# State space input of a three-branch trunk: projected channel-major and re-laid through DRAM in place of token-major with every eighth token stationary

## The chip, the cores and the metric

One core of a Trainium2 chip runs the whole kernel in one launch. The metric is the device time of one execution in microseconds (us). A core has five instruction queues: TensorE (PE, matrix products; its weight loads are a row of their own, PEld), VectorE (DVE), ScalarE (ACT), GpSimd (POOL) and SyncE (SP, which here only issues DMA transfers). Each engine works through its own instructions in the order of the program and waits on semaphores for the others.

## The reference

Two layers over 1024 tokens of 1024 channels. Each normalises its input, projects it with one matrix `w_in`, splits the columns among three mixers, gates each mixer's output, and adds the product with `w_out` to the residual. A is sparse attention with a top-256 selection of keys, B a state space layer on 256 of the columns (u), C latent attention. The change concerns u:

```python
proj = h @ w_in[l]
(qa, ka, va, iq, ik, iw, ga, u, gb, cq, ckv, kpe, gc) = jnp.split(proj, points, axis=-1)
ya = dsa_branch(qa, ka, va, iq, ik, iw, ...)
yb = s5_branch(u, ssm_a_re[l], ssm_a_im[l], ssm_b_re[l], ...)   # x_t = a x_(t-1) + B u_t; y = Re(C x) + D u
mixed = concat([ya * silu(ga), yb * silu(gb), yc * silu(gc)], axis=-1)
x = x + mixed @ w_out[l]
```

The 256 columns of u are 16 groups of 16 channels; each group drives a complex state of 64.

## The kernel before, in words

A layer starts by transposing the normalised input h into channel-major tiles, one for each block k of 128 input channels, split into two parts `hh` and `hl` (`h_hi[k]`, `h_lo[k]`, 128 channels x 1024 tokens). Weights arrive as `raw` by SP and are split by POOL into `whi` and `wlo`. Every product is the sum of three matmuls (hi x hi, lo x hi, hi x lo).

The projections run as a list of steps, `STEPS = "L5C6Q7U01234"` (line 52): L, C, Q and U are projections of 256 columns, the digits are gates of 128 columns. Two forms exist.

- Token-major, `proj` and `proj_step` (lines 723 to 754; matmuls on lines 730, 732, 733): a block of 128 tokens of h is the stationary operand, 256 columns of the weight move, and the result `pj` has tokens on the partitions. It takes 8 blocks of tokens x 8 blocks of channels x 3 = 192 matmuls of 256 columns. For step U the stationary block is not 128 neighbouring tokens but every eighth one, `slice(7 - e, 1024, 8)`, so that `pj` has chunk j of 8 tokens on the partitions. `ev_u` (line 763, ACT) copies it to two tiles `us[c]` with the chunk j on the partitions and (group, e, channel) along the row.
- Channel-major, `gates` (line 1122; matmuls of `mm3` on lines 167 to 169): the weight columns are stationary, 512 tokens move, and the result `gt` has channels on the partitions. It takes 2 halves x 8 x 3 = 48 matmuls of 512 columns for 128 columns of weight. A gate then goes by tanh (ACT, line 1132) and a product (DVE, line 1133) to the tile `gate`, is stored to the DRAM scratch `gate_d` (SP, line 1134), and comes back much later as `gin` (line 1238).

Beside this main stream run generators ("sides"). Every step of the main stream calls `tick` with an estimate of its time; a side whose next step is due then writes its instructions at that point of the program. So the order on each engine is set when the program is written, by these estimates. Three sides matter here.

- The selection of A's keys, `topk` (DVE mainly). Near its end a reduction gives `bad` (line 987), one matmul sums it over the partitions into `pb` (line 989), and DVE casts that to `badi` (line 991).
- The state space branch: `s5_tables`, then `s5` (line 356). `static(gh)` makes the tables of one half of the groups: `s5o` and `s5t` (DVE and POOL), small matmuls `tr<-zp,s5bd` and `tr<-s5o,s5bd` (line 397), the kernel `s5k` (line 405, DVE), eight SP transfers `s5m<-s5k` (line 409), and transposes of `s5t` (line 414). Then `chunks(gh)` (line 434) needs u as `U`, partitions (e, channel), rows (group, chunk): eight PE transposes of `us[gh]` (line 441) and two ACT copies (line 442) make it, and 16 small matmuls (line 449; the trace shows two records for each) give `vr` and `vi`, which DVE takes up on lines 457 and 458. `outputs(gh)` follows. The order is static(0), chunks(0), outputs(0) mixed with static(1), chunks(1), outputs(1).
- Attention of A: queries `qA` (DVE, line 1356, from PE transposes on line 1352 of `qa`, which SP loads on line 1346), scores (PE, lines 1360 and 1361), a maximum with the mask (DVE, line 1176), exponentials to `P` (ACT, line 1184), transposes of P (PE, line 1204) and the product with va into `acc_o` (line 1197).

Of the kernel before, what the change touches and what calls it, by code (L numbers as in the profile page):

```python
# [9 lines left out]
F32 = mybir.dt.float32  # L10
# [26 lines left out]
LEAD = 2  # L37
# [53 lines left out]
def hybrid_kernel(ctx, tc, A, out, dbg=None, layers=DEPTH):  # L91
# [31 lines left out]
    def scr(shape, dt, name):  # L123
        """scratch of up to 1, 2 or 4 KB a partition"""
        n = int(np.prod(shape[1:])) * (2 if dt == BF16 else 4)
        if n > 2048:
            return page(shape, dt, name)
        tag, bufs = ("k1", K1) if n <= 1024 else ("k2", K2)
        return sm.tile(shape, dt, tag=tag, name=name, bufs=bufs)
# [11 lines left out]
    # ---------------------------------------------------------------- constants  # L141
# [6 lines left out]
    # ---------------------------------------------------------------- helpers  # L148
# [12 lines left out]
    def rsq(o, x, c, m=1.0):  # L161
        """((x + c) * m) ** -0.5"""
# [8 lines left out]
    def rope(eng, o, x, c, s, t1, t2, dup=1):  # L171
        """x: [128, n, 2, h]; c, s: [128, h]; o: [128, n, dup, 2, h] or, without copies, [128, n, 2, h]"""
# [17 lines left out]
    # ---------------------------------------------------------------- state space branch  # L190
    zp = {}

    def tiny(name, n=8, dt=F32):
        """a slice of a page; the same name is the same place within a layer"""
# [8 lines left out]
    def exp_acc(x, name):  # L203
        """e ** x by 2 ** n and a polynomial; zero below the normal range"""
# [17 lines left out]
    def sincos(x, name):  # L222
# [17 lines left out]
        # quadrant  # L240
# [13 lines left out]
        # signs: sin is negative in quadrants 2, 3; cos in 1, 2  # L254
# [27 lines left out]
    def s5_tables(l, Z):  # L282
        """parameters of a layer: powers of abar, input matrices, rotation; as a generator"""
# [38 lines left out]
        # powers abar ** 0..8  # L322
# [17 lines left out]
        # e ** (8 i th), its powers of two, and the modulus of a chunk  # L340
# [15 lines left out]
    def s5(l, Z, us, yb):  # L356
        """groups 0..7, then 8..15; as a generator. The input must have been projected when sync is passed"""
# [6 lines left out]
        def table(eng, gh, name, e0, mr, mi):  # L364
            """[(group of the pair, state), re/im, pair, e, channel]: abar ** (e0 + e) * m"""
# [7 lines left out]
        def static(gh):  # L373
            """what the parameters give: input and output matrices, Toeplitz blocks, rotation"""
# [7 lines left out]
            # K[tau][c, c'] = Re(C abar ** tau B), both groups of a pair by block-diagonal matrices of input,  # L382
            # then the block Toeplitz matrices [(e c), g, (t c')]
# [17 lines left out]
            # D on the diagonal of tau = 0  # L401
# [15 lines left out]
            # rotation, unit modulus: e ** (8 i th j)  # L417
# [15 lines left out]

        def chunks(gh):
            """chunk inputs [(e c), g, j] and what they bring to the states"""
            h = H[gh]
            h["U"] = U = page([128, 8, 128], F32, "s5U")
            for q in range(2):
                p = ps_tr([128, 4, 128])
                for i in range(4):  # L440
                    T.transpose(p[:, i, :], us[gh][:, 4 * q + i].rearrange("p e c -> p (e c)"), ident)
                S.activation(U[:, 4 * q:4 * q + 4, :], p, AF.Copy)
                yield 1.5
# [25 lines left out]
            # states before each chunk  # L469
# [6 lines left out]
        def outputs(gh):  # L476
            """outputs [j, (t, g, c)], gelu (doubled), transposed to channels x tokens"""
# [30 lines left out]
        while len(us) < 3:  # L508
            yield 1.0
        yield from chunks(0)  # L510
# [7 lines left out]
        # g times the sigmoid of its linear layer (four times that)  # L518
# [25 lines left out]
    # work beside the main stream: generators that yield the time, in us, until their next step  # L544
# [3 lines left out]
    def side(gen, delay=0.0, behind=0):  # L548
        """behind: instructions that go first"""
# [19 lines left out]
    # ---------------------------------------------------------------- layers  # L569
    cq_d = dram.tile([2, 2, 128, 1024], F32, name="cq_d")  # L570
    qa_d = dram.tile([1024, 384], F32, name="qa_d")
    gate_d = dram.tile([8, 128, 1024], F32, name="gate_d")

# [1065 lines left out]
```

## Time and profile before

| | us |
|---|---|
| median of 3 runs | 1357.48 (1355.61 to 1359.18) |
| profiled execution, its span | 1357.0 |
| PE busy in it | 1306.3 |
| DVE busy | 919.6 |
| POOL busy | 681.7 |
| ACT busy | 666.5 |

The span is that of one profiled execution. A row of the timeline gives start, duration, engine, line, operation, output<-input; a number in square brackets is the idle time of the engine just before it, and what released it. A letter q behind an engine's name (SPq) marks the issue of a transfer by that engine's queue. Matmuls are pipelined: the duration of one is longer than the distance to the next, so the distance between starts is what one costs. PEclk in a table of stretches is the granted clock of PE as a share of full speed (1.00 is 2.4 GHz, 0.50 is 1.2 GHz).

### The profile page before, as it was taken

The page shows a single profiled execution, that of the slowest core. Times are in us where ns is not written, and L with a number is a line of the kernel's source. Part 1 is how long each engine was busy: PE and PEld are TensorE (multiplying, and loading weights), DVE is VectorE, ACT ScalarE, POOL GpSimd, SP SyncE. Part 2 cuts the span into 40 slices and gives each one's busy share as a digit, 9 for nine tenths or more (in the row PEclk, how much of TensorE's full clock was granted, in tenths as well). Part 3 has the DMA queues.
Part 4 walks back from the last instruction along what each step waited for, and adds up shares of the span by engine and source line. Part 5 has one row for each costly group of instructions (what it writes and reads, how often), then busy time and mean ns, then how long its engine had stood idle before and what let it go on. Part 6 is the DMA issues. An engine that isn't in the chain of part 4 may idle for free. (4 is left out here: it accounts for less than half of the span.)

```text
span 1357.0 us, 26056 instructions
## 1 busy us (share of the span) xinstructions
PE 1306.3 (96%) x9636; PEld 1153.7 (85%) x9636; DVE 919.6 (68%) x2672; ACT 666.5 (49%) x1521; POOL 681.7 (50%) x1109
## 2 busy tenths in 40 slices
PE   6999999999999999999999899999999999999998
PEld 6987899877788787789999789998777878777998
DVE  4478799698677866731253888978986776587211
ACT  5356621115788666751143674101277966668300
POOL 5987278255327743523158944843751476344400
PEclk8999999999999899999999899999999999999999
DMA  7102222112200001421150014222140100015103
GB/s 247 33 5 75 94 86 70 36 64 93 73 16 27 5 23 48 161 94 25 70 165 1 24 56 125 63 63 65 56 133 11 32 11 18 10 48 195 55 1 125
DMA packets 74849, 88.14 MB, mean 65 GB/s; under 512 B 12960, under 2 KB 62240, under 8 KB 74720
## 3 DMA queue, kind: packets, MB, share of 16 engines
q1 hardware_dynamic: 73568, 82.26, 19.1%
q0 software_dynamic: 1152, 4.19, 0.9%
q8 instruction: 76, 1.25, 0.4%
q14 instruction: 53, 0.43, 0.1%
HBM read 61.14 MB, written 24.12 MB: 63 GB/s over the span
## 5 line engine op out<-in xcount | busy, mean ns | idle before, releaser
L730 PE MATMUL pj<-whi,hh 128*128 128x256 f32 (+1 forms) x736 | 224.6, 305 | 0.9 <-POOL whi L150 0.9
L732 PE MATMUL pj<-wlo,hh 128*128 128x256 f32 (+1 forms) x736 | 223.7, 304 | 1.6 <-POOL wlo L151 1.6
L733 PE MATMUL pj<-whi,hl 128*128 128x256 f32 (+1 forms) x736 | 223.6, 305 | 0.0
L155 POOL TENSOR_TENSOR wlo<-raw,whi 128x1024 fp32r<-128x1024 f32 (+1 forms) x40 | 94.6, 2380 | 145.3 <-PE po L1470 65.8
L732 PEld LDWEIGHTS pj<-wlo,hh 128*128 128x128 f32 x736 | 160.6, 218 | 2.5 <-POOL wlo L151 1.8
L730 PEld LDWEIGHTS pj<-whi,hh 128*128 128x128 f32 x736 | 160.5, 218 | 2.2 <-POOL whi L150 1.2
L733 PEld LDWEIGHTS pj<-whi,hl 128*128 128x128 f32 x736 | 160.1, 218 | 0.3
L1469 PE MATMUL po<-whi,mix 128*128 128x256 f32 x512 | 145.2, 284 | 0.3 <-DVE xn L1556 0.3
L1470 PE MATMUL po<-wlo,mix 128*128 128x256 f32 x512 | 144.7, 284 | 0.0
L1471 PE MATMUL po<-whi,mix 128*128 128x256 f32 x512 | 143.9, 283 | 0.0
L1556 DVE TENSOR_TENSOR xn<-xn,po 128x256 f32<-128x256 f32 x64 | 26.4, 420 | 126.2 <-PE po L1471 126.2
L167 PE MATMUL gt<-hh,whi 128*128 128x512 f32 x256 | 103.9, 406 | 0.0
L169 PE MATMUL gt<-hh,wlo 128*128 128x512 f32 x256 | 102.5, 400 | 0.0
L168 PE MATMUL gt<-hl,whi 128*128 128x512 f32 x256 | 102.5, 400 | 0.0
L922 DVE SCALAR_TENSOR_TENSOR acc<-rl,iw,acc 128x384 f32<-128x384 f32 (+5 forms) x84 | 94.0, 1120 | 12.2 <-ACT rl L917 9.3
L1210 ACT ACTIVATE pt<-s 128x512 f32<-128x512 f32 (+1 forms) x154 | 82.6, 559 | 36.3 <-PE s L1204 30.0
L1469 PEld LDWEIGHTS po<-whi,mix 128*128 128x128 f32 x512 | 98.3, 192 | 0.7 <-DVE xn L1556 0.7
L1470 PEld LDWEIGHTS po<-wlo,mix 128*128 128x128 f32 x512 | 98.3, 192 | 0.0
L1471 PEld LDWEIGHTS po<-whi,mix 128*128 128x128 f32 x512 | 97.7, 192 | 0.0
L1204 PE MATMUL s<-ident,P 128*128 128x128 f32 x588 | 96.5, 281 | 0.6 <-ACT P L1184 0.2
L1184 ACT ACTIVATE P<-P,nb,qsc 128x1024 f32<-128x1024 f32 (+7 forms) x96 | 82.3, 865 | 21.8 <-DVE nb L1182 21.8
L1184 ACT ACTIVATE P<-P,nb,asum 128x1024 f32<-128x1024 f32 (+7 forms) x96 | 82.6, 868 | 17.6 <-DVE nb L1182 17.5
(447 smaller groups left out, 3660.8 us busy)
## 6 DMA issues: line engine op xcount, KB each, us to landing
raw<-in_w_in SPq DMA_DIRECT2D x32, 512.0 KB, 4.6
gate_d<-gate SPq DMA_DIRECT2D x16, 512.0 KB, 2.9
gin<-gate_d SPq DMA_DIRECT2D x16, 512.0 KB, 3.4
raw<-in_w_out SPq DMA_DIRECT2D x16, 512.0 KB, 4.6
x<-in_x SPq DMA_DIRECT2D x8, 512.0 KB, 5.4
cq_d<-cqs SPq DMA_DIRECT2D x16, 256.0 KB, 2.1
cqT<-cq_d POOLq DMA_DIRECT2D x8, 512.0 KB, 5.4
xn<-in_x SPq DMA_DIRECT2D x8, 512.0 KB, 9.3
```

The lines of the kernel that those rows point to most:

```text
L155: (eng or G).tensor_tensor(lo, raw, f(hi), op=ALU.subtract)
L167: T.matmul(ps, lh, rh, start=start, stop=False)
L168: T.matmul(ps, lh, rl, start=False, stop=False)
L169: T.matmul(ps, ll, rh, start=False, stop=stop)
L730: T.matmul(o, hk, hi[:, k, 0:n], start=kh == 0 and i == 0 and k == 0, stop=False, skip_group_check=True)
L732: T.matmul(o, hk, lo[:, k, 0:n], start=False, stop=False, skip_group_check=True)
L733: T.matmul(o, lk, hi[:, k, 0:n], start=False, stop=kh == 1 and k == 3, skip_group_check=True)
L1184: S.activation(Ps[j][:, 0:nk], Ps[j][:, 0:nk], AF.Exp, bias=nb[:, j:j + 1], scale=it["scale"][:, j:j + 1], accum_out=sums[:, j:j + 1])
L1204: T.transpose(p[:, i, :], Ps[j][:, 128 * kt:128 * kt + 128], ident)
L1469: T.matmul(o, mh, hi[:, k, :], start=first and i == 0 and k == 0, stop=False, skip_group_check=True)
L1470: T.matmul(o, mh, lo[:, k, :], start=False, stop=False, skip_group_check=True)
L1471: T.matmul(o, ml, hi[:, k, :], start=False, stop=final and k == 3, skip_group_check=True)
```

## The change

Step U now uses the channel-major form. The body of `gates` becomes a generator, `channels()`, used by the gates and by a new `inputs_s5()`: for each half c of the 256 columns, 48 matmuls of 512 columns give u with channels on the partitions; ACT copies each half of the tokens to a tile `uT` so that the eight tokens of a chunk come apart (position s, then chunk j), and SP stores the tile to a new DRAM scratch `u_d[c]`. The weight for step U is loaded as two blocks of 128 columns (`gate_w`) instead of two halves of 512 input channels; the bytes are the same.

In `s5` a new `inputs(gh)` loads `U` from that scratch by eight SP transfers of 64 KB, one for each position e: 16 partitions (channels) x 8 groups x 128 chunks. Both halves are asked for after static(0) and ahead of chunks(0). `chunks` loses its transposes and copies and the two yields of 1.5 between them; the `us` list holds only numbers of halves that are stored. The argument `sl` of `proj` goes. Comments go as well; they are left out here.

```diff
         def chunks(gh):
             h = H[gh]
-            h["U"] = U = page([128, 8, 128], F32, "s5U")
-            for q in range(2):
-                p = ps_tr([128, 4, 128])
-                for i in range(4):
-                    T.transpose(p[:, i, :], us[gh][:, 4 * q + i].rearrange("p e c -> p (e c)"), ident)
-                S.activation(U[:, 4 * q:4 * q + 4, :], p, AF.Copy)
-                yield 1.5
+            U = h["U"]
...
+        def inputs(gh):
+            H[gh]["U"] = U = page([128, 8, 128], F32, "s5U")
+            src = u_d[gh].rearrange("(g c) (s j) -> c g s j", c=16, s=8)
+            for e in range(8):
+                nc.sync.dma_start(U[16 * e:16 * e + 16, :, :], src[:, :, 7 - e, :])
...
         yield from static(0)
-        while len(us) < 3:
+        while len(us) < 2:
             yield 1.0
+        inputs(0)
+        yield 4.0
+        inputs(1)
         yield from chunks(0)
...
+    u_d = dram.tile([2, 128, 1024], F32, name="u_d")
...
+            elif x == "U":
+                reqs.extend(lambda col=col: gate_w(l, col) for col in (1192, 1320))
...
-        def ev_u(tp, ps):
-            if tp == 0:
-                us.extend(page([128, 8, 8, 16], F32, f"u{c}") for c in range(2))
-            for c in range(2):
-                S.activation(us[c].rearrange("p g e c -> p e g c")[:, 2 * tp:2 * tp + 2],
-                             ps[:, :, 128 * c:128 * c + 128].rearrange("p e (g c) -> p e g c", g=8), AF.Copy)
-            if tp == 3:
-                us.append(True)
...
-        def gates(c):
-            hi, lo, _ = ws.get()
-            g = page([128, 1024], F32, f"gate{c}")
-            for hf in range(2):
-                cs = slice(512 * hf, 512 * hf + 512)
-                ps = ps_s([128, 512], "gt")
-                for k in range(8):
-                    mm3(ps, hi[:, k, :], lo[:, k, :], h_hi[k][:, cs], h_lo[k][:, cs], k == 0, k == 7)
-                    tick(0.64)
+        def channels():
+            hi, lo, _ = ws.get()
+            for hf in range(2):
+                cs = slice(512 * hf, 512 * hf + 512)
+                ps = ps_s([128, 512], "gt")
+                for k in range(8):
+                    mm3(ps, hi[:, k, :], lo[:, k, :], h_hi[k][:, cs], h_lo[k][:, cs], k == 0, k == 7)
+                    tick(0.64)
+                yield hf, cs, ps
+        us = []
+        def inputs_s5():
+            for c in range(2):
+                u = page([128, 8, 128], F32, "uT")
+                for hf, _, ps in channels():
+                    S.activation(u[:, :, 64 * hf:64 * hf + 64], ps.rearrange("p (j s) -> p s j", s=8), AF.Copy)
+                nc.sync.dma_start(u_d[c], u.rearrange("p s j -> p (s j)"))
+                us.append(c)
+        def gates(c):
+            g = page([128, 1024], F32, f"gate{c}")
+            for hf, cs, ps in channels():
...
-                proj(ev_u, sl=lambda e: slice(7 - e, 1024, 8), outer=x not in INNER)
+                inputs_s5()
```

Since the estimates of the sides' due times change, so does the order on the engines. PE's instructions fall from 8534 to 8310. In the first layer, pb stood behind 192 matmuls of U and 12 of gate 0, and stands behind 96 of U and 16 of gate 0.

On PE, where vr and vi of the first half are made, the order of before. Names: s are scores, u_2786 the tile us[0], s5w the input matrices, tr a PSUM tile of transposes; line 1360 and 1361 make a pair.

```order
1636 L414 MATMUL tr<-ident,s5t 128x128 x4
1637 L1352 MATMUL tr<-ident,qa 128x128 x3
1638 L1360 MATMUL s<-ka_hi,qA 128x512
1639 L1361 MATMUL s<-ka_lo,qA 128x512
1640 L441 MATMUL tr<-ident,u_2786 128x128 x4
1641 L1360 MATMUL s<-ka_hi,qA 128x512
1642 L1361 MATMUL s<-ka_lo,qA 128x512
1643 L1360 MATMUL s<-ka_hi,qA 128x512
1644 L1361 MATMUL s<-ka_lo,qA 128x512
1645 L441 MATMUL tr<-ident,u_2786 128x128 x4
1646 L449 MATMUL vr<-s5U,s5w 64x128
1647 L449 MATMUL vi<-s5U,s5w 64x128
```

The same place on PE in the changed kernel (line 1372 is 1360 of before, 1373 is 1361, 450 is 449, 1364 is 1352).

```order
1540 L414 MATMUL tr<-ident,s5t 128x128 x4
1541 L1364 MATMUL tr<-ident,qa 128x128 x3
1542 L1372 MATMUL s<-ka_hi,qA 128x512
1543 L1373 MATMUL s<-ka_lo,qA 128x512
1544 L1372 MATMUL s<-ka_hi,qA 128x512
1545 L1373 MATMUL s<-ka_lo,qA 128x512
1546 L1372 MATMUL s<-ka_hi,qA 128x512
1547 L1373 MATMUL s<-ka_lo,qA 128x512
1548 L450 MATMUL vr<-s5U,s5w 64x128
1549 L450 MATMUL vi<-s5U,s5w 64x128
1550 L450 MATMUL vr<-s5U,s5w 64x128
1551 L450 MATMUL vi<-s5U,s5w 64x128
```

The transposes of u are gone. Five pairs of scores stand ahead of the first row in both. Before, ten pairs in all stood ahead of the last seven of the eight pairs of vr and vi, and two pairs behind them; now all eight follow the eighth pair of scores without a break, and four pairs of scores stand behind them. For the second half, vr and vi stand some 65 instructions earlier in the stream than before.

On SP, the queue around the s5m transfers, before:

```order
69 L409 DMA s5m<-s5k 16x8x32
70 L409 DMA s5m<-s5k 16x8x16
71 L1134 DMA gate_d<-gate_4001 128x1024
72 L1238 DMA gin_4141<-gate_d 128x1024
73 L1238 DMA gin_4143<-gate_d 128x1024
74 L1346 DMA qa<-qa_d 128x384 x2
```

And in the changed kernel:

```order
69 L409 DMA s5m<-s5k 16x8x32
70 L409 DMA s5m<-s5k 16x8x16
71 L1146 DMA gate_d<-gate_3904 128x1024
72 L1250 DMA gin_4044<-gate_d 128x1024
73 L1250 DMA gin_4046<-gate_d 128x1024
74 L439 DMA s5U<-u_d 16x8x128 x16
75 L1358 DMA qa<-qa_d 128x384 x2
```

Sixteen loads (eight for each half) have come in between the gin loads and the qa loads, behind all eight s5m transfers.

## Rows read from the trace of the kernel before

**Rows 1.** Page, part 1: engine, busy us (share of span), instructions.

```profile
PE 1306.3 (96%) x9636; PEld 1153.7 (85%) x9636; DVE 919.6 (68%) x2672; ACT 666.5 (49%) x1521; POOL 681.7 (50%) x1109
```

**Rows 2.** Stretches: us, busy (instructions) of PE, PEld, DVE, ACT, POOL; PEclk; DMA; GB/s.

```profile
202.00:248.00 46.00, 46.00 (x193) 45.97 (x191) 37.90 (x100) 5.18 (x10) 29.58 (x32) 1.00 0.17 52
248.00:300.00 52.00, 52.00 (x233) 42.79 (x233) 46.06 (x188) 8.66 (x14) 21.83 (x21) 1.00 0.16 53
```

**Rows 3.** Timeline of PE: first matmul of U, first gate matmul behind it.

```profile
202.25 0.29 PE L730 MATMUL pj<-whi,hh 128*128 128x256 f32 x1
...
248.40 0.40 PE L167 MATMUL gt<-hh,whi 128*128 128x512 f32 x1
```

**Rows 4.** Timeline of PE: two gate matmuls, six apart, in gate 7.

```profile
194.77 0.39 PE L167 MATMUL gt<-hh,whi 128*128 128x512 f32 x1
...
196.13 0.39 PE L167 MATMUL gt<-hh,whi 128*128 128x512 f32 x1
```

**Rows 5.** Timeline of DVE at the end of the selection; the last in layer 1.

```profile
236.53 0.15 DVE L987 TENSOR_REDUCE bad<-tk_ok 128x1 f32<-128x6 f32 x1
...
251.48 0.15 DVE L991 CAST badi<-pb 1x1 int32<-1x1 f32 x1 [10.80 <-PE pb L989]
...
918.15 0.15 DVE L991 CAST badi<-pb 1x1 int32<-1x1 f32 x1 [10.80 <-PE pb L989]
```

**Rows 6.** Timeline of PE from pb to the transposes of P.

```profile
251.26 0.19 PE L989 MATMUL pb<-consts,bad 128*1 128x1 f32 x2
...
304.86 0.63 PE L414 MATMUL tr<-ident,s5t 128*128 128x128 f32 x4 [2.82 <-DVE qA L1356]
...
312.02 0.39 PE L1360 MATMUL s<-ka_hi,qA 128*128 128x512 f32 x1
...
319.26 0.45 PE L449 MATMUL vr<-s5U,s5w 128*64 128x128 f32 x4
319.53 0.40 PE L449 MATMUL vi<-s5U,s5w 128*64 128x128 f32 x4
...
322.20 0.38 PE L1204 MATMUL tr<-ident,P 128*128 128x128 f32 x2
322.93 0.44 PE L1204 MATMUL tr<-ident,P 128*128 128x128 f32 x2 [0.35 <-ACT P L1184]
```

**Rows 7.** Groups of PE by line: busy us, mean ns, idle before.

```profile
L441 PE MATMUL tr<-ident,u 128*128 128x128 f32 x32 | 4.9, 276 | 0.0
```

**Rows 8.** Stretches behind two idle times of PE, columns as in rows 2.

```profile
307.00:308.00 1.00, 1.00 (x9) 1.00 (x8) 0.86 (x7) 0.00 (x0) 0.77 (x5) 0.50 0.07 16
...
446.00:456.00 10.00, 8.83 (x40) 7.83 (x42) 7.51 (x28) 6.62 (x13) 7.33 (x6) 0.50 0.00 0
```

**Rows 9.** Timeline of DVE: the kernel s5k is finished.

```profile
311.37 0.27 DVE L405 TENSOR_TENSOR s5k<-s5k,zp 16x128 f32<-16x128 f32 x1
```

**Rows 10.** Timeline of SP's queue: two zp loads, s5m, and what follows it.

```profile
262.10 0.43 SPq L290 DMA_DIRECT2D zp<-in_ssm_b_re  x1
262.58 0.43 SPq L290 DMA_DIRECT2D zp<-in_ssm_b_im  x1
...
311.70 5.22 SPq L409 DMA_DIRECT2D s5m<-s5k  x8
...
318.96 0.91 SPq L1346 DMA_DIRECT2D qa<-qa_d  x2
```

**Rows 11.** DMA issues: count, KB each, median us from issue to landing.

```profile
cqT<-cq_d POOLq DMA_DIRECT2D x8, 512.0 KB, 5.4
...
s5m<-s5k SPq DMA_DIRECT2D x4, 64.0 KB, 2.3
...
zp<-in_ssm_b_re SPq DMA_DIRECT2D x2, 64.0 KB, 1.9
```

**Rows 12.** Timeline of PE: the wait ahead of the slow stretch.

```profile
446.48 0.48 PE L1197 MATMUL acc_o<-pt,va 128*64 128x128 f32 x2 [1.98 <-DVE gin L1227]
```

More of the change, by code (lines that the diff above doesn't have):

```diff
@@ L613, in gate_w @@
         return raw, 128
-    R_U, R_IQ, R_K = [(1192, 1448)], [(512, 768)], [(384, 512), (768, 808), (2088, 2120)]
+    R_IQ, R_K = [(512, 768)], [(384, 512), (768, 808), (2088, 2120)]
     R_L, R_CQ, R_QA = [(1960, 2088), (0, 128)], [(1704, 1960)], [(128, 384)]
@@ L619, in in_weights @@
     def in_weights(l):
-        cols = dict(K=R_K, I=R_IQ, L=R_L, C=R_CQ, Q=R_QA, U=R_U)
+        cols = dict(K=R_K, I=R_IQ, L=R_L, C=R_CQ, Q=R_QA)
         reqs = []
@@ L721, in proj_halves, with proj_step @@
                             evac(2 * hf + p, pss[p])
-        def proj_step(ps, t0, kh, hi, lo, n, sl=None):
+        def proj_step(ps, t0, kh, hi, lo, n):
             for i in range(2):
                 t = t0 + i
-                cs = slice(128 * t, 128 * t + 128) if sl is None else sl(t)
+                cs = slice(128 * t, 128 * t + 128)
                 for k in range(4):
@@ L734, in proj_step, with proj @@
             tick(n / 100.0)
-        def proj(evac, sl=None, tps=range(4), outer=True):
+        def proj(evac, tps=range(4), outer=True):
             if not outer:
@@ L741, in proj @@
                     for kh in range(2):
-                        proj_step(ps, 2 * tp, kh, *w[kh], sl)
+                        proj_step(ps, 2 * tp, kh, *w[kh])
                     evac(tp, ps)
@@ L751, in proj @@
                     ps = pss[tp]
-                    proj_step(ps, 2 * tp, kh, hi, lo, n, sl)
+                    proj_step(ps, 2 * tp, kh, hi, lo, n)
                     if kh == 1:
                         evac(tp, ps)
-        us = []
-        def ev_u(tp, ps):
-            if tp == 0:
-                us.extend(page([128, 8, 8, 16], F32, f"u{c}") for c in range(2))
-            for c in range(2):
-                S.activation(us[c].rearrange("p g e c -> p e g c")[:, 2 * tp:2 * tp + 2],
-                             ps[:, :, 128 * c:128 * c + 128].rearrange("p e (g c) -> p e g c", g=8), AF.Copy)
-            if tp == 3:
-                us.append(True)
         iraw = {}
@@ L1117, in ev_g5 @@
             qa_out(tp, 2, ps)
-        mixf = {}
-        def gates(c):
+        def channels():
             hi, lo, _ = ws.get()
-            g = page([128, 1024], F32, f"gate{c}")
             for hf in range(2):
@@ L1130, in gates @@
                     tick(0.64)
+                yield hf, cs, ps
[7 more added lines that the diff above has]
+                us.append(c)
+        mixf = {}
+        def gates(c):
+            g = page([128, 1024], F32, f"gate{c}")
+            for hf, cs, ps in channels():
                 th = scr([128, 512], F32, "th")
```

## The prediction

> **What bounds the kernel now.** I read the page's engine shares first, then the stage that the change touches in a table of stretches, then PE, DVE and SP in order of time from there to the point where the new data is used. PE is busy for 96% of the span [rows 1], so the first question is how much PE work goes. The second, which decides here, is what PE waits for when it arrives early.
>
> The stage of U (state space input) is pure PE: 46.00 of 46.00 us, and weight loads fill 45.97 of it [rows 2]. Its 192 matmuls take from 202.25 to the first gate matmul at 248.40, 0.240 us each [rows 3], although they move only 256 columns; a gate matmul moves 512 and six take 194.77 to 196.13, 0.227 each [rows 4]. So U is bound by loading its strided stationary.
>
> Around that stage DVE is the other engine near its limit: 46.06 of 52 us in the stretch behind it [rows 2], and 3.5 of the idle rest lies ahead of 251.48. DVE runs the top-256 selection beside U and has `bad`, the input of the small matmul pb, ready at 236.53 + 0.15 = 236.68. PE reaches pb only at 251.3 [rows 6], and DVE stands for 10.80 us until then [rows 5]. So up to pb PE is late, and DVE waits for it. Further on it turns: PE stands 2.82 us for qA from DVE at 304.86 [rows 6]. Layer 1 repeats all this 666.67 us later (the same 10.80 at 918.15 [rows 5]), so I work one layer and double it.
>
> **What goes on PE.** Removed: 192 matmuls, 248.40 - 202.25 = 46.15 us. Added: 96 matmuls of the gate's form and loop, 96 x 0.227 = 21.8 us. That is -24.4 us. Removed too: 16 transposes of u, half of 4.9 us over both layers [rows 7], so -2.4. In full 26.8 us of PE per layer; if all reached the end, 1357.0 - 53.6 = 1303. The evacuations by ACT, the stores of uT and the same number of weight bytes lie beside PE work, as those of the gates do; they cost nothing while PE is in the gates.
>
> **First give-back: pb.** In the new order 96 + 16 matmuls stand ahead of pb, so PE is there at 202.25 + 112 x 0.227 = 227.7. `bad` still comes at 236.68, as nothing ahead of it on DVE moves. PE waits 9.0 us (nothing else is queued to pass pb) and goes on at 236.9, 14.4 earlier than 251.3. DVE loses its 10.80 us of idle, no more. From there to qA, DVE is nearly full, so qA comes 10.8 earlier, at 294.06 in place of 304.86. PE, 14.4 earlier, would be ready for it at 304.86 - 2.82 - 14.4 = 287.6, and waits about 6.5 where it waited 2.82. The work from there to the first scores took 312.02 - 304.86 = 7.16 us, partly at a granted clock of 0.50 [rows 6, 8]; a longer wait ahead may add 1 to 1.5 us of that. I take the first scores 10 us earlier (9.3 to 10.8), at 302.0. If nothing more were late, the gain would be 10 + 1.6 = 11.6 per layer, and the kernel at 1334.
>
> **Second give-back: U comes late.** Before, U was made on the chip between scores (transposes, ACT copies), and vr and vi (32 short records of PE) were mixed with ten pairs of scores. Now eight pairs and two groups of transposes stand ahead of all of them, about 4.3 us from the first scores, so PE is at vr at 302.0 + 4.3 = 306.3. vr needs eight loads of 64 KB from the new scratch. They stand on SP's queue behind the eight s5m transfers, a gate store and two gin loads. The s5m transfers wait for s5k, which DVE finishes at 311.37 + 0.27 [rows 9]; in the run before SP began them at 311.70 and was through with s5m, store and gin at 318.96, 7.26 us later [rows 10]. All of that moves by the 10 us of DVE: 301.7 to 309.0. No row shows the new loads. Their issue lies between 0.47 (two zp loads of 64 KB start 0.48 apart) and 0.65 each (5.22 / 8 for s5m) [rows 10], 3.8 to 5.2 us for eight; the landing lies between 1.9 (zp) and 2.3 (s5m), both 64 KB [rows 11]. U is there between 314.7 and 316.5, with the error of the shift between 313.9 and 317.2. I take 315.6, the middle, since the new loads resemble both rows. So PE stands about 9.3 us in front of vr, and most of the 10 us is given back. Behind these eight stand the other half's eight and then the two qa loads that later scores need; 16 issues end at 309.0 + 7.5 to 10.4, 316.5 to 319.4, about where the qa loads were before (318.96 [rows 10]), so they cost nothing.
>
> The Trainium skill, "DMA: Bandwidth & Descriptors", section "Rules for kernel authors", says to issue a DMA early, compute, and wait on it late, and to merge small transfers into a large one. Against this the change issues eight pieces, behind 7 us of other issues, though the scratch is written some 60 us earlier. By that rule, if the loads were issued early, the sum would end at the 1334 above; as the loads stand now it ends where the next paragraph puts it.
>
> **From U to the next common point.** That is the first transpose of P, at 322.20 before. Left to do are vr and vi, 32 x 0.0675 = 2.2 us (four take 319.26 to 319.53), and four pairs of scores, 8 x 0.227 = 1.8 [rows 4, 6]: 4.0 us at full clock. But PE comes from a long idle time. After 2.82 us of idle the clock still stood at 0.50 at 307 to 308; after a wait of 1.98 at 446.48 it was 0.50 for the whole 446 to 456 [rows 8, 12]. All at half clock is 7.9 us. I take about 3.5 us at half clock, as after the wait for qA, so 5.75 us: P's transposes start at 321.35, 0.85 earlier than now. P itself is ready long before, so the wait of 0.35 at 322.93 [rows 6] goes as well. The second half's chunk, whose loads are long there, saves its eight transposes, 1.2 us. Per layer that is 0.85 + 0.35 + 1.2 = 2.4, in both layers 4.8. Best end: 313.9 + 4.0 = 317.9, a gain of 4.3 + 1.55 = 5.85 per layer. Worst: 317.2 + 7.9 = 325.1, a loss of 2.9 - 1.55 = 1.35. DVE's L457, which needs vr, comes some 1.5 us earlier in the middle case, so it holds nothing up.
>
> The profiled execution has 1357.0 and the median of the runs is 1357.48, so I add 0.5: 1357.5 - 4.8 is 1352.7. Rounded towards the gains that L457 may hand on, 1352; its own range is 1345.8 to 1360.2.
>
> **Rivals.**
> (a) U isn't late. If SP got at the loads before s5m, or PE's other work covered them, the 10 us stay: 1334. Against it speaks the queue's order, which is written in the program. Chance 0.06, the 1303 of the full saving included.
> (b) A later stall goes too. At 446.48 PE stands 1.98 us for DVE, and then runs 10 us at half clock [rows 8, 12], 8.83 busy, of which 4.4 is the clock. In the new order the second half's vr and vi come some 65 PE instructions earlier, so attention items and gates meet differently there. If the stall and its slow clock vanish, 6.4 per layer go with them: 1352 - 12.8 = 1339. For it: it is one coincidence of POOL, DVE and PE. Against: such a coincidence can as well form anew. Chance 0.17.
> (c) Slower: the loads land late and PE wakes up slowly. Place: the wait ahead of vr. If the loads take 0.65 to issue and land after 5.4 us, like the 512 KB cqT [rows 11] (16 of them are in a row, 1 MB in all, with s5m and gin just ahead), U is there at 309.0 + 5.2 + 5.4 = 319.6, and with 7.9 us at half clock P starts at 327.5. That is 5.3 late, less 1.55: +3.75 per layer, 1365. It decides from U at about 318.0 with my 5.75 us (no gain left), and from 317.9 at half clock throughout (2 us lost per layer). The Trainium skill, "TensorE: Matmul & The Clock Gate", section "HAM oscillation — how this bites in real kernels", describes just this: short bursts of matmuls with DMA waits between them stay cold. The rows on 307 and 446 agree; by them the half-clock end is real. Chance 0.17.
> (d) Nothing is left: U at 318 and no more, the second half's transposes hidden anyway. 1357. Chance 0.08.
> That the new matmuls are not faster is excluded as far as a trace can: they are the gate's loop, in the gate's shapes, at 0.227.
>
> **How the numbers follow.** Forecast 0.52, (a) 0.06, (b) 0.17, (c) 0.17, (d) 0.08. Within 0.3% (4.1 us, about what a measurement of this kernel can tell from no change) is 1353.4 to 1361.5. The forecast's range, 1345.8 to 1360.2, puts some 0.33 of its 0.52 below 1353.4 and 0.19 inside. Faster: 0.33 + 0.06 + 0.17 = 0.56. Same: 0.19 + 0.08 = 0.27. Slower: 0.17. The range goes from 1338, which takes in (b), to 1362, the lower part of (c).
>
> **What would show it.** In the new profile: U's stage 21 to 22 us long; PE idle of 8 to 10 us in front of pb with DVE's idle of 10.80 gone; the wait for qA longer than 2.82; a wait of 8 to 11 us on the s5U loads in front of vr, at about 306 to 316, and a granted clock of 0.5 after it; P's first transposes within 2 us of 322.20. PE busy falls by some 50 us while the span falls by about 5. It is wrong if U lands before 310 or after 319, if DVE from pb to qA doesn't move by about 10.8, or if the stretch 440 to 460 changes by more than 3 us.

## The result, and the profile after

The changed kernel takes 1377.15 us in the median against 1357.19 for the kernel before, measured beside it: a ratio of 1.0147, with a 95% interval of 1.0121 to 1.0172. It is slower by some 20 us; 1352 was predicted, with a range of 1338 to 1362. The profiled execution spans 1374.5 us, 17.5 more than the one before. Its part 1 of the page, in the columns of [rows 1]:

```profile
span 1374.5 us, 25661 instructions
...
PE 1265.8 (92%) x9412; PEld 1098.4 (80%) x9412; DVE 935.8 (68%) x2672; ACT 662.4 (48%) x1505; POOL 682.1 (50%) x1109
```

PE lost 40.5 us of busy time and gained 58 us of waiting. The list of what PE waited for (total us over both layers, times, longest) says on what. The first three are of this place in the program; none of them took as much as 0.5 us before. The last four belong to the stretch that comes up below:

```profile
PE vr L450 <- DMA s5U<-u_d: 25.4, 2, 12.9
PE pb L984 <- DVE bad L982: 22.4, 2, 11.2
...
PE tr L397 <- POOL s5bd L390: 6.3, 4, 2.6
PE s L1348 <- DVE qr L1331: 5.2, 2, 2.6
...
PE acc_o L1209 <- DVE pt L1224: 4.2, 2, 3.4
PE s L1348 <- DVE P L1186: 4.2, 1, 4.2
...
PE acc_o L1209 <- DVE gin L1239: 1.8, 6, 0.4
```

So far this is what was forecast: a wait at pb, then one at vr. The timeline of PE in layer 0, to be read beside [rows 6] (line 984 is 989 of before, 1372 is 1360, 450 is 449, 1216 is 1204):

```profile
237.28 0.19 PE L984 MATMUL pb<-consts,bad 128*1 128x1 f32 x2 [11.21 <-DVE bad L982]
...
296.26 0.63 PE L414 MATMUL tr<-ident,s5t 128*128 128x128 f32 x4 [1.04 <-DVE qA L1368]
...
301.02 0.39 PE L1372 MATMUL s<-ka_hi,qA 128*128 128x512 f32 x1
...
318.99 0.82 PE L450 MATMUL vr<-s5U,s5w 128*64 128x128 f32 x4 [12.95 <-DMA s5U<-u_d]
...
324.28 1.03 PE L1216 MATMUL tr<-ident,P 128*128 128x128 f32 x8
```

pb comes 14.0 earlier and the first scores 11.0 earlier. Then PE stands 12.95 us in front of vr, and the transposes of P come at 324.28 instead of 322.20. The place where the loss is must be sought further on, since 2 us per layer don't make 17.5. To find it I follow one instruction through all kernels: the matmul that closes a head pair of A or C (`acc_o<-ident,rb`, line 1223, 96 of them). The table gives its start before, and how much later it starts elsewhere. Each row is from one profiled execution (that of e1, 1376.65 us, lies 8 below e1's median, that of e6, 1367.8, lies 5 above its own); the runs are introduced below.

| kernel | 1st | 21st | 29th | 47th (end of layer 0) | 69th (the 21st of layer 1) | 95th (end of layer 1) |
|---|---|---|---|---|---|---|
| before, start in us | 330.30 | 437.82 | 483.36 | 596.60 | 1104.79 | 1264.29 |
| changed kernel | +1.5 | +1.5 | +13.4 | +8.8 | +11.6 | +17.3 |
| e1, early loads | -7.9 | -8.4 | +12.7 | +8.7 | +1.1 | +17.7 |
| e3, early loads, late chunk | -4.8 | -5.3 | -4.9 | -5.0 | -9.8 | -10.3 |
| e4, before with neighbouring tokens | -7.6 | -7.6 | -8.2 | -8.2 | -13.8 | -12.4 |
| e5, mix on DVE | +3.8 | +3.7 | +12.7 | +5.9 | +8.5 | +11.6 |
| e6, before with mix on DVE | -0.2 | -0.1 | +3.8 | +3.6 | +8.2 | +9.0 |
| e7, late chunk only | -1.0 | -2.0 | +6.6 | +2.2 | +2.1 | +5.5 |
| e8, e3 with pb late | -7.0 | -7.2 | -8.2 | -7.9 | -14.1 | -15.2 |
| e9, e3 with mix on DVE | -2.1 | -2.6 | -2.6 | -3.9 | -10.7 | -9.9 |
| e10, before with early chunk | +0.7 | 0.0 | +27.2 | +25.1 | +25.1 | +47.8 |
| e11, early loads, place 349 | -4.9 | -5.2 | +6.1 | +1.4 | -3.6 | +2.5 |
| e12, early loads, place 406, pb late | -9.0 | -12.0 | -2.6 | -3.7 | -12.6 | -7.3 |

In the changed kernel everything up to 438 costs 1.5 us. Between the 21st and the 29th, 438 to 483 us in the time of before, 12 us are lost, of which 4.6 come back by the 47th; in layer 1 the same stretch (69th to 95th) loses 5.7. That is the start of C's items, far behind U. The stretch from the 21st to the 29th, of the kernel before and then of the changed kernel (columns as [rows 2]):

```profile
437.82:483.36 45.54, 41.69 (x332) 34.68 (x331) 36.29 (x116) 29.92 (x78) 33.37 (x52) 0.89 0.03 7
```

```profile
439.29:496.80 57.51, 49.88 (x364) 40.94 (x362) 44.68 (x127) 35.84 (x90) 30.83 (x52) 0.88 0.05 16
```

PE's idle time grows from 3.9 to 7.6 us, and its time at half clock from some 10 to some 14 us (a mean clock of 0.89 and 0.88 over the stretch). Another 32 matmuls stand in it, most of them taken from the work behind it, so a part of the loss comes back. The wait for gin of [rows 12] has shrunk to 0.4 at most; the list of the kernel before has it as

```profile
PE acc_o L1197 <- DVE gin L1227: 3.8, 2, 2.0
```

Longer ones stand in its place. Timeline of PE:

```profile
448.90 0.66 PE L1348 MATMUL s<-kc0h,qT 104*128 104x384 f32 x1 [2.60 <-DVE qr L1331]
...
459.84 0.58 PE L1348 MATMUL s<-kc0h,qT 104*128 104x256 f32 x1 [4.17 <-DVE P L1186]
```

What holds DVE there is in its own timeline, with POOL's beside it (second fence):

```profile
454.22 2.39 DVE L1194 SCALAR_TENSOR_TENSOR nb<-mx,qsc 128x2 f32<-128x2 f32 x1
456.53 2.65 DVE L1297 TENSOR_TENSOR kt<-kt,kr__6017 128x256 f32<-128x256 f32 x1
...
460.80 1.97 DVE L1298 TENSOR_TENSOR kt<-kr,kr__6017 128x128 f32<-128x128 f32 x1
462.70 1.48 DVE L1297 TENSOR_TENSOR kt<-kt,kr__6017 128x256 f32<-128x256 f32 x1
```

```profile
454.23 4.67 POOL L155 TENSOR_TENSOR mix<-gin,mix 128x1024 fp32r<-128x1024 f32 x2
...
460.26 2.36 POOL L155 TENSOR_TENSOR mix<-gin,mix 128x1024 fp32r<-128x1024 f32 x1
462.59 2.71 POOL L279 TENSOR_TENSOR s5tab<-s5z,s5R 128x508 f32<-128x508 f32 x2
```

The kt operations took 0.41 (128x256) and 0.28 (128x128) in the kernel before:

```profile
450.81 0.41 DVE L1285 TENSOR_TENSOR kt<-kt,kr__6093 128x256 f32<-128x256 f32 x1
451.14 0.28 DVE L1286 TENSOR_TENSOR kt<-kr,kr__6093 128x128 f32<-128x128 f32 x1
```

In the changed kernel each ends 0.15 to 0.3 us after POOL's operation ends: 456.53 + 2.65 = 459.18 behind POOL's 454.23 + 4.67 = 458.90, 460.80 + 1.97 = 462.77 behind 462.62. The one of 128x2, 0.24 before, ends with the first of POOL's two. Together these four lose some 7 us of DVE. The Trainium skill, "SBUF — State Buffer", section "Who interferes with whom", says that a DVE instruction with two inputs in SBUF contends with a GpSimd instruction that reads SBUF, since they share a read port; these rows agree. (In the kernel before, the mix splits lay at 443, 448 and 453 and held only one DVE operation for long, nb at 443.52 with 1.90.)

### The profile page after: what moved, and what is told of

It reads as the page before. It is cut to its first block, busy times and chain, and to the rows that moved or that the text cites. A ratio compares the mean times of both kernels' runs of the same rounds, so it can differ in the third digit from the quotient of the medians.

```text
span 1374.5 us, 25661 instructions
## 1 busy us (share of the span) xinstructions
PE 1265.8 (92%) x9412; PEld 1098.4 (80%) x9412; DVE 935.8 (68%) x2672; ACT 662.4 (48%) x1505; POOL 682.1 (50%) x1109
## 5 line engine op out<-in xcount | busy, mean ns | idle before, releaser
L737 PE MATMUL pj<-whi,hh 128*128 128x256 f32 (+1 forms) x608 | 172.1, 283 | 0.6 <-POOL whi L150 0.6
L739 PE MATMUL pj<-wlo,hh 128*128 128x256 f32 (+1 forms) x608 | 170.8, 281 | 1.6 <-POOL wlo L151 1.6
L740 PE MATMUL pj<-whi,hl 128*128 128x256 f32 (+1 forms) x608 | 170.8, 282 | 0.0
L167 PE MATMUL gt<-hh,whi 128*128 128x512 f32 x320 | 132.4, 414 | 0.0
L169 PE MATMUL gt<-hh,wlo 128*128 128x512 f32 x320 | 131.0, 409 | 0.0
L168 PE MATMUL gt<-hl,whi 128*128 128x512 f32 x320 | 130.9, 409 | 0.0
L739 PEld LDWEIGHTS pj<-wlo,hh 128*128 128x128 f32 x608 | 116.2, 191 | 2.5 <-POOL wlo L151 1.8
L737 PEld LDWEIGHTS pj<-whi,hh 128*128 128x128 f32 x608 | 116.2, 191 | 1.7 <-POOL whi L150 0.8
L740 PEld LDWEIGHTS pj<-whi,hl 128*128 128x128 f32 x608 | 115.8, 191 | 0.3
L1186 DVE TENSOR_SCALAR_CACHE_REDUCE P<-s 128x512 f32<-128x512 f32 (+3 forms) x144 | 75.5, 549 | 16.5 <-PE s L1350 15.7
```

The lines of the kernel that those rows point to most:

```text
L167: T.matmul(ps, lh, rh, start=start, stop=False)
L168: T.matmul(ps, lh, rl, start=False, stop=False)
L169: T.matmul(ps, ll, rh, start=False, stop=stop)
L737: T.matmul(o, hk, hi[:, k, 0:n], start=kh == 0 and i == 0 and k == 0, stop=False, skip_group_check=True)
L739: T.matmul(o, hk, lo[:, k, 0:n], start=False, stop=False, skip_group_check=True)
L740: T.matmul(o, lk, hi[:, k, 0:n], start=False, stop=kh == 1 and k == 3, skip_group_check=True)
```

## The experiments

What was to be told apart: whether the loss comes from U's late loads, from the place to which the state space chunk of the second half has moved, or from POOL's hold on DVE there. "Place" below is the number of PE rows of the program between the first vr of the first half and that of the second: 417 before, 368 with the change. Counted in PE records of the traces the same distance is 1069 (8 transposes of u among them) and 987 (958 in e1, 1061 in e3).

**e1: ask for the first half early.**

```diff
-        yield from static(0)
         while len(us) < 2:
             yield 1.0
         inputs(0)
-        yield 4.0
+        yield from static(0)
         inputs(1)
```

> The changed kernel, with the eight loads of U for the first half asked for at the start of the state space side, right after the tables' loads, instead of behind the s5m transfers; nothing else is edited. Theory: the wait of 12.95 us for s5U in front of vr (and the half clock behind it) is what the changed kernel gives back first, and it is only the queue's order. Then PE meets vr without a wait, the transposes of P come some 11 us earlier than in the changed kernel, and the time falls by about 22 us over two layers, to about 1355. Rival: something else holds the same place (DVE's first scores, or the tables on POOL), a wait of another name appears within 15 us, and the time stays above 1368.

Measured: 1384.36 us (1376.65 to 1389.55), ratio 1.0197 (1.0165 to 1.0230), where the theory had 1355. That nothing else is edited doesn't hold either: the edit also takes out the `yield 4.0` ahead of the chunks. The wait did go, and 9.4 us came back (+1.5 to -7.9 in the table), as the theory says:

```profile
305.71 1.09 PE L450 MATMUL vr<-s5U,s5w 128*64 128x128 f32 x16
```

No bracket: PE meets vr without waiting. But between the 21st and the 29th matmul 21 us are lost, more than in the changed kernel. So late loads aren't all of the slowdown. But e1 doesn't measure them alone: with that yield gone the chunk has moved further forward, to place 327. PE's timeline in that stretch, and two pieces behind it (columns as [rows 2]):

```profile
479.52 0.80 PE L487 MATMUL s<-s5m,s5U 128*128 128x128 f32 x2 [3.11 <-DVE s5g L496]
```

```profile
480.00:484.00 4.00, 4.00 (x15) 2.88 (x14) 1.94 (x11) 1.92 (x4) 0.00 (x0) 0.50 0.00 0
...
488.00:492.00 4.00, 4.00 (x15) 3.20 (x14) 2.59 (x6) 1.83 (x3) 0.00 (x0) 0.50 0.01 2
```

The second half's outputs (line 487) wait here for DVE, and 12 us at half clock follow, 480 to 492.

**e3: e1, and the two yields of the chunks put back.**

```diff
         def chunks(gh):
             h = H[gh]
             U = h["U"]
+            yield 1.5
+            yield 1.5
             vr, vi = ...
```

> As e1_early_loads, and in addition the two yields of 1.5 that the change took out of the chunks are put back, so that vr and vi of the second half come again about where they stood before the change (400 PE rows behind those of the first half; 417 before the change, 368 with it, 327 in e1). Theory: the 7 us per layer lost between 440 and 468 come from the second half's chunk moving forward into that stretch; then this runs about 14 us faster than e1, near 1341. Rival: the loss there has nothing to do with where the chunk stands; then it runs like e1 within 4 us.

Measured: 1346.89 us, ratio 0.9903 (0.9878 to 0.9928). 37 us faster than e1 (28 between the two profiled executions), where 14 were expected, by three units of a number that only sets where instructions are written down. Nothing is lost between 438 and 483. The time is 6 above the 1341 of the theory.

**e10: the yields alone, in the kernel before.** This is one part of the change alone.

```diff
                 S.activation(U[:, 4 * q:4 * q + 4, :], p, AF.Copy)
-                yield 1.5
```

> The kernel before, with nothing but the two yields of 1.5 behind the transposes of u taken out, as the change takes them out. U is still projected token-major, and nothing goes through DRAM. vr of the second half then stands 367 to 379 PE rows behind that of the first half (417 before, 368 with the change). Theory: the place of the chunk alone costs what the changed kernel loses between 440 and 500, some 6 us per layer: about 1369. Rival: the place costs nothing by itself and needs the late loads to hurt; then 1357 within 4 us.

Measured: 1405.74 us, ratio 1.0347 (1.0327 to 1.0367): 48 us for the two yields, where 12 were expected; no instruction is added or removed, and only the order differs. It all comes behind the 21st matmul of each layer. The stretch from the 21st to the 47th in layer 0, of the kernel before and then of e10 (columns as [rows 2]):

```profile
437.82:596.60 158.78, 152.12 (x1222) 123.16 (x1220) 110.92 (x368) 106.73 (x261) 72.85 (x122) 0.97 0.21 71
```

```profile
437.82:621.70 183.88, 168.29 (x1243) 134.14 (x1241) 116.49 (x385) 112.90 (x274) 77.01 (x134) 0.93 0.19 65
```

Nearly the same matmuls (1222 and 1243) take 25.1 us longer. PE is idle for 15.6 instead of 6.7 us, 8.9 more. At a mean clock of 0.97 some 6% of the time is at half clock, at 0.93 some 14%: 26 us instead of 10, which costs 8 more. The last 8 are counted as busy (16.2 more in all); 21 more matmuls stand in the stretch, and what else is in the 8 these views don't part. So the order that the two yields set is a cause by itself. But e10 moves it further than the change does (below), so its 48 us isn't the price of the change's own order.

**e4: the faster projection alone, in the kernel before.**

```diff
-                proj(ev_u, sl=lambda e: slice(7 - e, 1024, 8), outer=x not in INNER)
+                proj(ev_u, outer=x not in INNER)
```

> The kernel before, with one edit: in step U the stationary block is 128 neighbouring tokens instead of every eighth, so u is permuted in time and the output of the state space branch isn't the reference's. No order changes, no DRAM. This measures what the strided stationary alone costs, without late loads. Theory: U takes 192 x 0.12 = 23 us, PE waits about 9 us at pb, the shift behind is bound by DVE at 8 to 10 us, and it ends near 1357 - 2 x 9 = 1339. Rival: other waits eat it and it ends above 1350.

Measured: 1346.31 us, ratio 0.9906 (0.9886 to 0.9926), 12.7 us faster. The first two matmuls of U in PE's timeline, and what PE waits for in the program:

```profile
200.75 0.28 PE L730 MATMUL pj<-whi,hh 128*128 128x256 f32 x1
200.86 0.28 PE L732 MATMUL pj<-wlo,hh 128*128 128x256 f32 x1
```

```profile
PE pb L989 <- DVE bad L987: 21.5, 2, 10.8
...
PE tr L414 <- DVE qA L1356: 6.8, 2, 3.6
PE tr L397 <- POOL s5bd L390: 6.2, 2, 3.2
```

Neighbouring tokens as stationary cost 0.12 us per matmul instead of the 0.240 of [rows 3]. PE saves 23 us per layer and gives 15 back at pb, at the tables and at qA. Layer 0 keeps 7.6 to 8.2, the lower end of the 8 to 10 that DVE and the tables were expected to leave, and layer 1 only 4.2; so the time lies 7 above the theory's 1339, and still below the rival's 1350.

**e8: e3, and pb written down 90 PE rows later.**

```diff
-            pb = ps_tr([128, 512], "pb")
-            T.matmul(pb[0:1, 0:1], bad, ones, start=True, stop=True)
-            badi = sm.tile([1, 1], I32, tag="badi", name="badi", bufs=1)
-            V.tensor_copy(badi, pb[0:1, 0:1])
...
+            (the same four lines, ahead of)
             yield IFT
             v = nc.values_load(badi[0:1, 0:1], ...)
```

> As e3_early_and_late_chunk, with the pb matmul and its cast written down at the end of the selection, 90 PE rows later. Theory: PE's wait of 11.2 us for bad goes, but DVE has no idle time left there and sets the end of the tables and qA, so the same wait comes back in front of the small matmuls of the tables and of qA, and the time stays within 4 us of e3's 1347. Rival: pb's place was what held PE; then some 10 us per layer are gained: about 1328.

Measured: 1344.44 us, ratio 0.9902 (0.9873 to 0.9930), the same as e3. The wait moved as expected, though to POOL's part of the tables rather than to qA:

```profile
PE tr L397 <- POOL s5bd L390: 34.2, 4, 16.7
```

So from pb to the scores the tables' chain (DVE and POOL) is the bound, and pb's place is not.

**e7: a later chunk, late loads kept** (`yield 4.0` between the two halves becomes `yield 6.0`; place 420).

> The changed kernel, with the wait of 4.0 between asking for the two halves raised to 6.0. The loads stay behind s5m, so the wait for U in front of vr stays; but everything behind it in the state space side comes later in the program, and vr of the second half stands 420 PE rows behind the first (417 before the change, 368 with it). Theory: the loss between 440 and 500 comes from the place of the second half's chunk; it goes, 7 us per layer, and the time is about 1360 with the 12.95 us wait still there. Rival: it is the late U that sets the rest off balance; then the time stays above 1370.

Measured: 1367.00 us, ratio 1.0071 (1.0043 to 1.0098). 10 us of the 20 come back, where 17 were expected. In the profiled executions 6.4 of it come ahead of the stretch (3.5 and 2.9 in the two layers: vr starts 1.6 us earlier in layer 0, and PE's wait there is 9.95), 5.4 in it: between the 21st and the 47th matmul 4.2 us are still lost, in the changed kernel 7.3. e3, at place 400 with early loads, is 20 us faster than this; half of that lies ahead of the stretch, where the loads are, and half in it.

**e11: early loads, place 349** (one `yield 2.0` ahead of vr).

> Between e1 and e3: early loads, one yield of 2.0 in front of vr, so that the second half's vr stands 349 PE rows behind the first (327 in e1, which took 1384; 400 in e3, which took 1347). Theory: the loss depends on where the chunk falls, and at 349 it still falls into the beginning of C's items: 1360 to 1380. Rival: any yield is enough to separate them; then it runs like e3, 1347 within 4 us.

Measured: 1361.88 us, ratio 1.0031 (1.0018 to 1.0044), between e1 and e3 as expected. With early loads the place orders the times: 327 gives 1384, 349 gives 1362, 400 gives 1347. In records of the trace the second half's vr stands 987 behind the first, exactly as in the changed kernel. So e11 is the run that parts the two causes (only the first half's outputs stand some 50 records earlier in it). With the same place it loses nearly the same in the stretch, 6.6 and 6.1 us against 7.3 and 5.7, and the early loads give 15 us (1377 to 1362), nearly all of it ahead of the stretch (6.7 and 7.8 in the two layers).

**e12: early loads, place 406, pb late** (one `yield 4.0`, and the edit of e8).

> The best that these runs point to: early loads, one yield of 4.0 in front of vr (the second half's vr stands 406 PE rows behind the first), pb written at the end of the selection. Theory: it runs like e8, 1344 within 4 us, since DVE and POOL still set the time of the tables. Rival: a place 6 rows on changes the stretch 440 to 500 by more than 4 us in either direction.

Measured: 1351.85 us, ratio 0.9950 (0.9934 to 0.9965), 7 us more than e8, whose chunk stands 4 rows from it (402). The rival holds here: e12 is 4.8 us ahead of e8 at the 21st matmul and loses 8.3 up to the 47th. Near the good place a few rows still change some us, so "later is better" isn't a rule.

**e5 and e6: the second part of the split of mix on DVE, in the changed kernel and in the kernel before.**

```diff
-                split_act(mixf[c], *mix[c])
+                split_act(mixf[c], *mix[c], V)
```

> The changed kernel, with the second part of the split of mix (POOL, 2.4 us each) computed on DVE instead. Theory: between 454 and 465 DVE's short operations (kt 2.65 instead of 0.41, nb 2.39 instead of 0.2) are held for as long as POOL's subtraction runs; with that off POOL they take 0.2 to 0.4 again and some 6 us per layer come back, less about 1.3 us of DVE for each split: about 1367. Rival: DVE is slow there for another reason; then the time stays at 1377 or grows.

> The control for e5: the kernel before, with the second part of the split of mix on DVE instead of POOL. Theory: holding DVE's short operations during POOL's subtraction hurts because the change moved the two together; before, only one operation was held there (nb, 1.90 us), so this gains at most 2 us per layer: 1354 to 1359. Rival: POOL's subtraction costs that much in any order; then this gains some 6 us like e5 and comes to 1352 or less.

Measured: e5 1371.49 us, ratio 1.0093 (1.0073 to 1.0112), 5.7 less than the changed kernel; e6 1362.75 us, ratio 1.0029 (1.0013 to 1.0044), 5.5 more than the kernel before. The same edit gains in one order and costs in the other; e6 meets neither its theory nor its rival. In e5 the loss from the 21st to the 47th matmul is 2.2 instead of 7.3 (3.1 instead of 5.7 in layer 1). But of the 12 us lost up to the 29th, where POOL's subtractions lay, 9.0 are still lost, and the split now takes DVE 1.2 to 2.3 us each. So POOL's hold may be a part of the loss in the changed kernel; its share isn't shown.

**e9: e3 with the same edit.**

> As e3_early_and_late_chunk, with the second part of the split of mix on DVE. Theory: with the chunk back at its place there is little left to gain from POOL, so 1344 to 1348. Rival: the hold by POOL costs as much there as in the changed kernel, and it runs 5 to 10 us faster, below 1341.

Measured: 1347.37 us, ratio 0.9915 (0.9886 to 0.9944), the same as e3. With the chunk at its place POOL has nothing to give.

**What the runs say of the order, together.** "C's first scores" is the first matmul `s<-kc0h,qT` of a layer. Its place among the head pairs, and the distance from it to the second half's vr, are the same in both layers of every run. The losses are differences of the table above.

| kernels | head pairs closed ahead of C's first scores | second half's vr, PE records behind (+) or ahead of (-) C's first scores | lost from the 21st to the 47th, us | lost from the 69th to the 95th, us |
|---|---|---|---|---|
| before, e4, e6 | 18 | +90 | 0, -0.6, 3.7 | 0, 1.4, 0.8 |
| e3, e8, e9 | 18 | +82 | 0.3, -0.7, -1.3 | -0.5, -1.1, 0.8 |
| e7, e12 | 19 | +81 | 4.2, 8.3 | 3.4, 5.3 |
| changed kernel, e11, e5 | 20 | -43 | 7.3, 6.6, 2.2 | 5.7, 6.1, 3.1 |
| e1 | 20 | -75 | 17.1 | 16.6 |
| e10 | 21 | -67 | 25.1 | 22.7 |

So the yields move two things at once: the second half's chunk comes earlier, from behind C's first scores to ahead of them, and C's first scores come later among the head pairs. No run moves one without the other. That the order in this stretch costs the time is shown; which of the two it is, isn't.

## Why the prediction was wrong, step by step

- **PE's saving.** Right. U's 96 matmuls run in the gate's form; e4 shows from the other side that the strided stationary made U slow (0.240 to 0.12). PE's busy time fell by 40.5 rather than 53; the mean granted clock fell with it (0.982 to 0.960 over the whole execution), so some of the rest ran slower.
- **pb.** Right: 11.21 us of waiting (9.0 forecast), PE 14.0 earlier (14.4). The sizes behind it were off on DVE's side. I had DVE 10.8 us earlier from there; the kernel s5k came 8.6 earlier (311.37 to 302.75), and so did qA (304.86 to 296.26). A DVE operation just ahead of `bad` and two just behind it lay under POOL's weight split and masks this time. The first (234.78 to 237.16, 2.38 us instead of 0.22) made `bad` itself 0.5 later, the other two cost some 3 us:

```profile
234.78 2.38 DVE L1015 TENSOR_SCALAR kp<-consts,tk_need 128x8 int32<-128x8 f32 x1
237.07 0.15 DVE L982 TENSOR_REDUCE bad<-tk_ok 128x1 f32<-128x6 f32 x1
237.14 1.87 DVE L1016 COPY_PREDICATED m<-kp,consts 128x8 f32<-128x8 int32 x1
...
239.65 1.45 DVE L1015 TENSOR_SCALAR kp<-consts,tk_need 128x8 int32<-128x8 f32 x1
...
302.75 0.36 DVE L405 TENSOR_TENSOR s5k<-s5k,zp 16x128 f32<-16x128 f32 x1
```

  (The operations of 1.87 and 1.45 took 0.15 and 0.22 before.) The idle 10.80 us of DVE had been idle of POOL as well; now both work there. That the first scores still came 11.0 earlier, where 9.3 to 10.8 were forecast, is luck: the work from qA to them took 4.76 us (296.26 to 301.02) instead of 7.16, most of it at full clock this time, and that made up for DVE.
- **U's readiness.** The mechanism was right, the size short: 318.99 instead of 315.6, beyond the worst end of 317.2. SP's queue shows where, with its own wait, the eighth of the loads, and the time to landing of all 16 (second fence):

```profile
303.18 5.22 SPq L409 DMA_DIRECT2D s5m<-s5k  x8
...
310.43 9.50 SPq L439 DMA_DIRECT2D s5U<-u_d  x16
...
SPq L439 <- DMA gin<-gate_d: 2.3, 2, 1.7
...
315.85 0.30 SPq L439 DMA_DIRECT2D s5U<-u_d  x1
```

```profile
DMA to landing us min/median/max: 2.3/3.0/5.8
```

  1.5 us is DVE's shift, as above. s5m, store and gin took 7.25 us, as before. Then two terms failed. The queue itself stood 2.3 us for the two gin loads (512 KB each, 4.7 and 6.2 us to landing), so the eighth load was issued only at 315.85, 5.4 us behind the first, where a queue without waits gives seven issues of 0.47 to 0.65. And the landing wasn't 1.9 to 2.3: the first seven loads, behind the gin loads, took 4.7 to 5.8 us, the eighth 3.0. I took 1.9 to 2.3 from rows whose transfers were almost alone. The kernel before had a row under the same traffic, the two qa loads behind the same two gin loads (318.96 in [rows 10]):

```profile
DMA to landing us min/median/max: 5.3/5.3/5.3
```

- **Half clock behind the wait.** Right: from 319 to 322 the granted clock was mostly 0.50, the lower level (0.65 in the last half us), and the 32 records of vr and vi took 3.3 us instead of 2.2. From U to P's transposes it took 5.3 us (5.75 forecast). With the late U that gives +2.1 us at the first common point (324.28 against 322.20), where -0.85 was forecast and +2.9 was the worst end; at the 1st matmul of the table it is +1.5.
- **"The second half's chunk saves its eight transposes, 1.2 us."** This is the step that failed, and it set the sign. The chunk did not stand there as before, less eight transposes. Without two yields it stands ahead of C's first scores instead of behind them, and C's first scores come two head pairs later. Instead of giving 1.2 us per layer the stretch cost 7.3 and 5.7 us in the changed kernel, and 25.1 and 22.7 in e10, which moves the order further. Of the 22 us between the forecast and the profiled execution (1352.2 and 1374.5) this stretch makes 15, and what lies ahead of it, the late U above all, makes 7. I saw that vr stood 65 rows earlier, and entered it as rival (b) only as a gain, "if the stall vanishes", with "such a coincidence can as well form anew" as a word against it. The stall did vanish: of the wait of 1.98 for gin at most 0.4 is left. New ones formed (2.6 for qr in each layer, 4.17 for P in layer 0, 3.4 for pt in layer 1), and the time grew. No price was put on that side, though the same rows (a wait of 1.98, 10 us at half clock) price it at +6 per layer as well as -6. The prediction's last sign of being wrong, a change of more than 3 us between 440 and 460, came true here: from the 21st to the 25th matmul, 437.8 to 458.5 in the time of before, the changed kernel falls back by 8.2 us.
- **Rival (c)** had the right sign for the wait ahead of vr. Its U at 319.6 is nearer to the measured 318.99 than the forecast's 315.6, in part by luck: it has 5.4 us of landing for the eighth load, which took 3.0, and no wait of the queue. It had too much half clock (7.9 us to P's transposes, where 5.3 were measured), so P came 2.1 late and not 5.3. And it sought the loss at vr, where only a part of it is: e11, without that wait, is still no faster than the kernel before.
- **Rival (a)**, 1334 if U isn't late: e3 and e8 are that kernel with the chunk in place, and end at 1347 and 1344. e8's 7.0 to 8.2 us in layer 0 fits the 8.6 that DVE and POOL allow; layer 1 gave 7.3, and e3 5 in each layer.

Put together from the runs: the faster projection is worth 13 us (e4). In the changed kernel late loads take 15 (e11 against it, at the same place), and the order in the stretch takes 13 (7.3 and 5.7). Putting the order back in part, with late loads, returns 10 (e7); early loads with the order put back are 30 us faster than the changed kernel (e3); early loads with the chunk still further forward return nothing (e1). Both repaired, the new projection is about 1% faster than the kernel before. What remains open is which part of the order matters, the chunk or C's first scores, and which single wait in 438 to 483: POOL's hold on DVE and the waits for the outputs are seen in the traces, their shares aren't shown.

## What to carry to other kernels

When an edit removes instructions from a side stream, look for the pacing that went with them: here two yields decided over 48 us (e10), and the projection over 13. Of work that moves by some rows into a stretch with waits, price both signs, and give the loss a chance like the gain. A load that is needed at a known point belongs in the queue ahead of the burst that waits for late data, and its landing time is to be read from a row under the same traffic. In an experiment that moves one thing, look in its trace whether it moved another: e1 was meant to move loads and moved the chunk too.

## What the runs showed of the hardware

- A DVE operation of 128x256 took 2.65 us instead of 0.41 while POOL operations of 2.36 us ran (changed kernel, 456.53), one of 128x2 took 2.39 instead of 0.24 (454.22); the first ended 0.28 us behind POOL's, the second with it. Others beside POOL, such as the maximum on line 1186 (0.68 at 460.19), weren't slowed.
- A stationary operand of every eighth element cost 0.240 us per matmul of 256 columns ([rows 3]), one of neighbouring elements 0.12 (e4), with the weight loads back to back in both.
- Loads of 64 KB landed 4.7 to 5.8 us after their issue right behind two loads of 512 KB, and 2.3 to 3.0 us when those had landed (changed kernel, 310 to 322), against 1.9 to 2.3 [rows 11].
